# A hybrid diffusion layer on one core: Exp of the cumulated decay taken from the rows broadcast for the decays

## The chip, the cores and the metric

The kernel runs on one core of a Trainium2 chip. A core has five engines that run side by side, each through its own instructions in their fixed order: TensorE (PE: matmuls from the on-chip memory SBUF into the accumulation memory PSUM), VectorE (DVE), ScalarE (ACT), GpSimd (POOL) and SyncE (SP, which issues the DMA transfers here). They wait for each other through semaphores. The metric is the device time of one execution in microseconds (us).

## What is computed

One layer of a diffusion backbone for 512 latent tokens and 128 context tokens (640 columns, in five chunks of 128), 1024 channels. The part that the change touches is the Mamba-2 scan, with 16 heads of 64 channels, in two directions (forward and backward, d = 0 and 1):

```python
a_cum = jnp.cumsum(dtc * a.reshape(g, r), axis=2)             # per chunk of 128 tokens
seg = a_cum[:, :, :, None] - a_cum[:, :, None, :]
decay = jnp.exp(jnp.where(lower, seg, -jnp.inf))
cb = jnp.einsum("bcign,bcjgn->bcijg", cc, bc)
y_diag = jnp.einsum("bcijg,bcijgr,bcjgrp->bcigrp", cb, decay, xdt)
...
y_off = jnp.einsum("bcign,bcgrpn,bcigr->bcigrp", cc, prev, jnp.exp(a_cum))
y = (y_diag + y_off).reshape(bsz, seqlen, h, p).astype(x.dtype)
```

Around it stand an adaLN modulation, an input projection `proj = h @ prm["w_in"]` whose columns feed the scan and a gated convolution of 31 taps (with a layer norm over its channels), an output projection of both joined, and a gated feed-forward part with a 3x3 convolution between two products.

## The kernel before

Channels lie on the 128 partitions, tokens along the free dimension (640 columns). Each large product is made from splits of both operands into a high and a low part, with three matmuls for each k, in two halves of 384 and 256 columns (`mm3`, L261 to L267). The weights come in units: SP loads `wr` (L141), ScalarE rounds `wh` (L165), mostly POOL subtracts `wl` (L167). Three units may be split ahead.

The 16 heads are handled as eight pairs (p = 0 to 7), two heads h to a tile of 128 channels. `ssd(p)` (L584) does one pair. For each head and direction it broadcasts the row of the cumulated decay over all 128 partitions by a matmul with a selection column of `idr` (L623), in two pieces q of 384 and 256 columns; ScalarE takes Relu of the difference to the token's own decay, chunk by chunk (L629; for d = 1 of the last pair VectorE does, L626), then Exp of the whole row (L637). VectorE or POOL multiplies by the masked products of C and B (L640). L658 multiplies the result with the tokens: `y_diag`. The other term, `y_off`, is C times the states (L647), times `ea` (L649), both directions added (L650), and added to the rest by `ssd_tail` (L674). `ea` is exp(a_cum) with the two heads' values on the partitions of their channels. The inner function `decays()` makes it: VectorE casts a selection matrix `sel` (L600), one matmul of 512 columns for each direction broadcasts the rows by it (L604), and ScalarE takes Exp of each (L608).

Where tiles lie matters for the rest. The tiles `slot("S10")` and `slot("S11")` hold `ea` of every pair in turn; a new one can be written when L650 and L674 of the pair before have read the old one. PSUM has three large tiles of two banks each (P0, P1, P2; `ps0` to `ps2` in the listings) and two small banks (Q0, Q1; `pq0`, `pq1`). Pairs 0 to 6 broadcast their rows into Q0 and Q1 in turn. The last pair broadcasts into P0 (d = 0) and P2 (d = 1). P2 also holds the sums of the 31-tap convolution (`conv31`, L713), P1 the layer norm's statistics (`ln_stats`, L742: mean, the differences L752, their squares L754, the root L332 and the SiLU L827), and P0 is where six of the eight "ahead" products (`ahead_parts`, L843 to L850: the output projection's part for pairs 0 to 4, 30 matmuls to a unit) are summed; two go to P2.

The program is written pair by pair, with the projections between them (`seq`, L181 to L211), but the order in which each engine runs it is set when the kernel is built: a scheduler takes instructions as its own model of time says that they will be ready, so any change of the code can move instructions elsewhere. The order is then fixed.

Of the kernel before, what the change touches and what calls it, by code (L numbers as in the profile page):

```python
# [8 lines left out]
F32R = mybir.dt.float32r  # L9
AF = mybir.ActivationFunctionType  # L10
# [3 lines left out]
P = 128  # L14
D = 1024
L = 512
# [31 lines left out]
def hybrid_layer_kernel(ctx: ExitStack, tc: tile.TileContext, xT, ct, prm, cst, wrest, wdt, idhl_d, wada1, wada2, win,  # L48
                        wout, wup, wdown, st0, yT, nsf, nsb):
    nc = tc.nc  # L50
    te, ve, ac, gp, sy = nc.tensor, nc.vector, nc.scalar, nc.gpsimd, nc.sync
# [3 lines left out]
    sm = ctx.enter_context(tc.tile_pool(name="sm", bufs=2))  # L55
# [4 lines left out]
    def nm(s):  # L60
        uid[0] += 1
        return f"{s}_{uid[0]}"

    def slot(tag, dt=F32, shape=(P, T)):
        return sb.tile(list(shape), dt, tag=tag, name=nm(tag))

    def psum(i):
        return ps.tile([P, 1024], F32, tag=f"P{i}", name=nm(f"ps{i}"))

    def psq(i):  # L70
        return ps.tile([P, 512], F32, tag=f"Q{i}", name=nm(f"pq{i}"))
# [4 lines left out]
    def prm_col(name, i=0, n=1):  # L76
        a = _COLS[name][0] + i
        return prms[:, a:a + n]
# [25 lines left out]
    ids = sb.tile([P, 32], F32, tag="idhl", name="ids")  # L104
# [87 lines left out]
    for p in range(NPAIR):  # L192
# [4 lines left out]
        last = p == NPAIR - 1  # L197
# [345 lines left out]
    def ssd_tokens(p):  # L543

        xs = xsp[p]
        xt = xtp[p] = slot(("S14", "T13", "S14", "T13", "S14", "M2", "S14", "M2")[p])
        to_tokens(xs, xt)
        xw = []
        for d in range(2):
            o = slot(f"S{4 + d}")  # L550
            gp.tensor_tensor(hq(o), hq(xt), WD[:, :, 16 * d + 2 * p:16 * d + 2 * p + 2].unsqueeze(3)
                             .to_broadcast([P, NCH, 2, 64]), MUL)
            xw.append(o)
        xwp[p] = xw
# [29 lines left out]
    def ssd(p):  # L584
        g = p // 4
        xs, xt, prev = xsp[p], xtp[p], prevs[p]
        last = p == NPAIR - 1
        xd = []
        for d in range(2):
            o = slot(("M4", "H11")[d] if last else f"S{2 + d}")  # L590
            a = 16 * d + 2 * p
            gp.tensor_tensor(hq(o), hq(xt), DT[:, :, a:a + 2].unsqueeze(3).to_broadcast([P, NCH, 2, 64]), MUL)
            xd.append(o)

        ea = []

        def decays():
            peas = []
            sel = sm.tile([P, 2, 2, 64], F32R, tag="sel", name=nm("sel"), bufs=1)
            ve.tensor_copy(sel, ids.rearrange("p (d h) -> p d h", d=2)[:, :, 2 * p:2 * p + 2]  # L600
                           .unsqueeze(3).to_broadcast([P, 2, 2, 64]))
            for d in range(2):
                pea = psq(d)
                te.matmul(pea[:, 0:L], sel[:, d].rearrange("p h q -> p (h q)"), acHL[:, 0:L], start=True, stop=True)  # L604
                ea.append(slot(f"S{10 + d}"))
                peas.append(pea)
            for o, pea in zip(ea, peas):
                ac.activation(o[:, 0:L], pea[:, 0:L], AF.Exp)  # L608

        if last:  # L610
            decays()

        rs = {}
        for h in range(2):
            for d in range(2):
                row = 2 * p + h + 16 * d
                sel1 = idr[:, row:row + 1].to_broadcast([P, P])
                r = slot(f"{'H' if last else 'S'}{(12 if last else 6) + 2 * h + d}")
                if last:
                    pbl = psum(2 * d)  # L620
                for q, (c0, c1) in enumerate(((0, 3), (3, 5))):
                    pb = pbl[:, 512 * q:512 * q + 512] if last else psq(q)
                    te.matmul(pb[:, 0:(c1 - c0) * P], sel1, acHL[:, c0 * P:c1 * P], start=True, stop=True)  # L623
                    for c in range(c0, c1):
                        if last and d:
                            ve.tensor_scalar(r[:, c * P:(c + 1) * P], pb[:, (c - c0) * P:(c - c0 + 1) * P],  # L626
                                             ACM[:, c, row:row + 1], 0.0, SUB, MIN)
                            continue
                        ac.activation(r[:, c * P:(c + 1) * P], pb[:, (c - c0) * P:(c - c0 + 1) * P], AF.Relu,  # L629
                                      scale=-1.0, bias=ACM[:, c, row:row + 1])  # L630
                rs[h, d] = r
        if p + 1 < NPAIR:
            ssd_tokens(p + 1)
        if not last:
            decays()
        for (h, d), r in rs.items():
            ssd_exp[0] = ac.activation(r, r, AF.Exp, scale=1.0 if last and d else -1.0)  # L637
        for i, (h, d) in enumerate(rs):
            r = rs[h, d]
            (ve if i % 2 or last else gp).tensor_tensor(r, r, cbm[g][d], MUL)  # L640
        if p + 1 < NPAIR:
            ssd_states(p + 1)

        for d in range(2):
            po = psq(d)
            for c in range(4):
                te.matmul(po[:, c * P:(c + 1) * P], prev[d][c if d == 0 else 3 - c],  # L647
                          cT[g][:, c * P:(c + 1) * P], start=True, stop=True)
            ve.tensor_tensor(ea[d][:, 0:L], ea[d][:, 0:L], po[:, 0:L], MUL)  # L649
        (ve if p > 5 else gp).tensor_tensor(ea[0][:, 0:L], ea[0][:, 0:L], ea[1][:, 0:L], ADD)  # L650

        t = slot(f"T{p}")
        for q, cc in enumerate(((0, 1, 2, 3), (4,))):
            py = psq(q)
            for i, c in enumerate(cc):
                for d in range(2):
                    for h in range(2):
                        te.matmul(py[64 * h:64 * h + 64, i * P:(i + 1) * P],  # L658
                                  xd[d][:, c * P + 64 * h:c * P + 64 * h + 64],
                                  rs[h, d][:, c * P:(c + 1) * P], start=d == 0, stop=d == 1,  # L660
                                  tile_position=(0, 64 * h))
            c0, c1 = cc[0] * P, (cc[-1] + 1) * P
            ve.scalar_tensor_tensor(t[:, c0:c1], xs[:, c0:c1], prm_col("d_skip", p), py[:, 0:c1 - c0], MUL, ADD)
        yoff[p] = ea[0]
        tp[p] = t
# [105 lines left out]
    for it in seq:  # L771
        if it[0] == "proj":
            n = it[1]
# [3 lines left out]
            elif n[0] == "a":  # L777
                p = int(n[1:])
# [10 lines left out]
            elif n[:2] == "xs":  # L789
                p = int(n[2:])  # L790
# [12 lines left out]
        elif it[0] == "ssd":  # L803
            p = it[1]
# [362 lines left out]
    for i in range(HEAD, 2 * NF):  # L1167
        q, half = ups[i]
# [243 lines left out]
```

## Time and profile before

| | us |
|---|---|
| median of 3 runs | 1036.93 (1034.02 to 1041.4) |
| the profiled execution, whole | 1034.38 |
| its span on the core | 1032.6 |
| first part (norm, modulation, first projections) | 0 to about 80 |
| input projections and scan | about 80 to 422 |
| output projection and what follows | 422 to the end |

The whole execution is 1.8 us longer than the span, the time in which instructions run. In the listings, a group or line is named by its line in the kernel, the engine, the operation, and the tiles it writes and reads (out<-in, with their shape). Where idle time stands behind a row, it is that of the engine just before it, with what ended it.

### The profile page before, as it was taken

The numbers are of one execution on the slowest core, as the hardware profiler recorded it, in microseconds if no ns is written. First come the engines' busy times: TensorE is split into PE (matmuls) and PEld (weight loads), VectorE is DVE, ScalarE is ACT, GpSimd is POOL, SyncE is SP. The second block draws the span as 40 slices with busy tenths as digits, with TensorE's granted clock in tenths as the row PEclk, the third lists the DMA queues.
The fourth block names the chain that finished last, engine by engine and source line by source line (L and its number), as shares of the span: only waits on it lengthen the run. The fifth ranks groups of instructions, "written<-read, shape, count | busy, mean of one in ns | idle before, by whom it ended". The sixth has DMA issues, their size and how long they took to land. (4 is left out here: it accounts for less than half of the span.)

```text
span 1032.6 us, 18800 instructions
## 1 busy us (share of the span) xinstructions
PE 974.4 (94%) x7655; PEld 939.6 (91%) x7655; DVE 755.0 (73%) x1117; ACT 451.6 (44%) x750; POOL 574.3 (56%) x402
## 2 busy tenths in 40 slices
PE   4999999999999899999989969989999998999995
PEld 2799999999899888999889969989999998999995
DVE  3689999989999988762585999998888889200004
ACT  6244648565374677723455522323233336222221
POOL 3333878879778785543661535584444444344444
PEclk9999999999999999999999989989999999999998
DMA  9622222222111111588462311122222221222212
GB/s 344 233 67 78 68 72 63 72 67 68 52 62 57 50 39 47 196 293 292 133 207 86 121 62 62 63 68 76 82 64 81 83 81 55 62 90 72 68 46 102
DMA packets 42934, 102.76 MB, mean 100 GB/s; under 512 B 4832, under 2 KB 12768, under 8 KB 42848
## 3 DMA queue, kind: packets, MB, share of 16 engines
q1 hardware_dynamic: 42848, 101.56, 29.6%
q8 instruction: 60, 0.98, 0.4%
q14 instruction: 26, 0.21, 0.1%
HBM read 97.87 MB, written 3.67 MB: 98 GB/s over the span
## 5 line engine op out<-in xcount | busy, mean ns | idle before, releaser
L167 POOL TENSOR_TENSOR wl<-wr,wh 128x1024 fp32r<-128x1024 f32 (+3 forms) x127 | 301.8, 2378 | 306.5 <-ACT wh L165 300.5
L267 PE MATMUL ps<-H,wh 128*128 128x384 f32 (+1 forms) x1664 | 327.1, 310 | 4.9 <-DVE M L413 2.2
L267 PE MATMUL ps<-T,wh 128*128 128x384 f32 (+1 forms) x1504 | 283.9, 310 | 14.2 <-DVE S L1085 14.1
L165 ACT ACTIVATE wh<-wr 128x1024 fp32r<-128x1024 f32 (+3 forms) x131 | 131.6, 1005 | 335.9 <-PE ps L267 236.1
L267 PEld LDWEIGHTS ps<-H,wh 128*128 128x128 f32 x1664 | 253.0, 188 | 9.3 <-issue 4.5
L267 PEld LDWEIGHTS ps<-T,wh 128*128 128x128 f32 x1504 | 227.7, 190 | 15.3 <-issue 14.8
L1082 DVE SCALAR_TENSOR_TENSOR S<-ps,prms,S 128x441 f32<-128x441 f32 (+2 forms) x288 | 197.2, 692 | 28.4 <-ACT S L1072 22.1
L713 DVE SCALAR_TENSOR_TENSOR ps<-u,prms,ps 128x655 f32<-128x655 f32 x223 | 200.7, 900 | 9.9 <-ACT ps L710 5.4
L267 PE MATMUL ps<-H,wl 128*128 128x384 f32 (+1 forms) x832 | 197.9, 309 | 0.0
L267 PE MATMUL ps<-T,wl 128*128 128x384 f32 (+1 forms) x752 | 172.3, 309 | 0.0
L267 PEld LDWEIGHTS ps<-H,wl 128*128 128x128 f32 x832 | 130.9, 188 | 1.6 <-issue 1.4
L267 PEld LDWEIGHTS ps<-T,wl 128*128 128x128 f32 x752 | 116.8, 189 | 0.0
L333 DVE RECIPROCAL rsm<-rsm 128x160 f32<-128x160 f32 (+2 forms) x9 | 7.3, 815 | 145.4 <-ACT rsm L332 145.4
L267 PE MATMUL ps<-S,wh 128*128 128x384 f32 (+1 forms) x448 | 93.5, 315 | 4.0 <-DVE S L1085 3.3
L267 PEld LDWEIGHTS ps<-S,wh 128*128 128x128 f32 x448 | 71.0, 191 | 6.6 <-issue 4.7
L267 PE MATMUL ps<-S,wl 128*128 128x384 f32 (+1 forms) x224 | 58.3, 312 | 1.2 <-POOL wl L167 1.2
L629 ACT ACTIVATE S<-pq,ACM 128x128 f32<-128x128 f32 x140 | 40.9, 373 | 18.3 <-PE pq L623 18.1
L1082 DVE SCALAR_TENSOR_TENSOR S<-S,prms,S 128x441 f32<-128x441 f32 (+2 forms) x48 | 45.8, 984 | 1.2 <-ACT S L1072 1.1
L267 PEld LDWEIGHTS ps<-S,wl 128*128 128x128 f32 x224 | 37.6, 190 | 1.6 <-POOL wl L167 1.6
L1072 ACT ACTIVATE S<-ps,prms 128x640 f32<-128x640 f32 x36 | 31.3, 868 | 0.0
L1164 POOL TENSOR_TENSOR H<-S,S 128x640 f32<-128x640 f32 x16 | 26.0, 1622 | 3.3 <-DVE S L1085 3.3
L580 POOL TENSOR_TENSOR S<-S,stmp 128x128 f32<-128x128 f32 x36 | 18.6, 517 | 15.1 <-ACT S L569 11.2
(345 smaller groups left out, 1238.1 us busy)
## 6 DMA issues: line engine op xcount, KB each, us to landing
wr<-in_wup SPq DMA_DIRECT2D x44, 512.0 KB, 3.4
wr<-in_win SPq DMA_DIRECT2D x36, 512.0 KB, 3.4
T<-in_wada SPq DMA_DIRECT2D x49, 256.0 KB, 5.6
wr<-in_wdown SPq DMA_DIRECT2D x16, 512.0 KB, 3.4
wr<-in_wout SPq DMA_DIRECT2D x13, 512.0 KB, 3.4
H<-in_wada SPq DMA_DIRECT2D x23, 256.0 KB, 5.5
S<-in_wada SPq DMA_DIRECT2D x16, 256.0 KB, 5.5
wr<-in_wdown SPq DMA_DIRECT2D x8, 384.0 KB, 3.1
```

Source lines behind the costliest of these rows:

```text
L165: ac.activation(hi[:, :n], raw[:, :n], AF.Copy)
L167: lo_eng.tensor_tensor(lo[:, :n], raw[:, :n], hi[:, :n].bitcast(F32), SUB)
L267: last_mm[0] = te.matmul(pt[:, o:o + c1 - c0], w, x[:, c0:c1], start=first and i == 0, stop=last and i == 2)
L333: ve.reciprocal(r[:, 0:seg], r[:, 0:seg])
L580: gp.tensor_tensor(now, now, tmp, ADD)
L629: ac.activation(r[:, c * P:(c + 1) * P], pb[:, (c - c0) * P:(c - c0 + 1) * P], AF.Relu, scale=-1.0, bias=ACM[:, c, row:row + 1])
L713: ve.scalar_tensor_tensor(acc, u[:, j:j + UO], w(j), acc, MUL, ADD)
L1072: ac.activation(out, v, AF.Identity, bias=prm_col("ffn_b", i), scale=w(1, 1))
L1082: ve.scalar_tensor_tensor(ob, vl[:, r0 + a - 1:r1 + a - 1, q0 + b - 1:q1 + b - 1], w(a, b), ob, MUL, ADD)
L1164: gp.tensor_tensor(f_raw[q], a, b, MUL)
```

## The change

`decays()` goes, and with it the tile `sel`, its cast, the two selection matmuls of each pair and the two Exp of 512 columns. `ea` is taken instead from the rows that L623 broadcasts anyway: after the Relus on one piece of a row of head h and direction d, ScalarE takes Exp of the same PSUM bank on the 64 partitions of that head, for the columns of the latent tokens only: 384 in the first piece, 128 in the second. Each pair so has eight Exp of 64 partitions in place of two of 128. The slots S10 and S11 are taken at the start of `ssd`. For d = 1 of the last pair VectorE and ScalarE both read the row from PSUM.

```diff
-        ea = []
-
-        def decays():
-            peas = []
-            sel = sm.tile([P, 2, 2, 64], F32R, tag="sel", name=nm("sel"), bufs=1)
-            ve.tensor_copy(sel, ids.rearrange("p (d h) -> p d h", d=2)[:, :, 2 * p:2 * p + 2]
-                           .unsqueeze(3).to_broadcast([P, 2, 2, 64]))
-            for d in range(2):
-                pea = psq(d)
-                te.matmul(pea[:, 0:L], sel[:, d].rearrange("p h q -> p (h q)"), acHL[:, 0:L], start=True, stop=True)
-                ea.append(slot(f"S{10 + d}"))
-                peas.append(pea)
-            for o, pea in zip(ea, peas):
-                ac.activation(o[:, 0:L], pea[:, 0:L], AF.Exp)
-
-        if last:
-            decays()
+        ea = [slot(f"S{10 + d}") for d in range(2)]
...
                         ac.activation(r[:, c * P:(c + 1) * P], pb[:, (c - c0) * P:(c - c0 + 1) * P], AF.Relu,
                                       scale=-1.0, bias=ACM[:, c, row:row + 1])
+                    n = min(c1, 4) - c0
+                    hp = slice(64 * h, 64 * h + 64)
+                    ac.activation(ea[d][hp, c0 * P:(c0 + n) * P], pb[hp, 0:n * P], AF.Exp)
                 rs[h, d] = r
         if p + 1 < NPAIR:
             ssd_tokens(p + 1)
-        if not last:
-            decays()
```

The build gives the engines another order, mostly in small exchanges. The large move is at the end of the scan. Line numbers in the listings are those of each kernel's own file; in the changed one L608 is the row broadcast (L623 before), L614 the Relu (L629), L618 the new Exp, L623 the Exp of the row (L637), L633 the product with the states (L647), L836 the eviction of an ahead product (L850).

TensorE before, right after the last input projection: pair 7's rows for d = 0 go into P0 (`ps0_515`, `ps0_519`) between the work of pairs 5 and 6.

```order
L604 MATMUL pq1_424_3554<-HL_87_657,sel_421_3549 128x512
L623 MATMUL ps0_515_4279<-HL_87_657,idr_601 128x256
L565 MATMUL pq0_426_3567<-S4_419_3545,M7_292_2606 128x128 x3
L567 MATMUL pq0_426_3567<-M7_292_2606,S4_419_3545 128x128
L565 MATMUL pq1_428_3575<-S5_420_3547,M7_292_2606 128x128 x3
L567 MATMUL pq1_428_3575<-M7_292_2606,S5_420_3547 128x128
L623 MATMUL ps0_519_4297<-HL_87_657,idr_601 128x384
L647 MATMUL pq0_436_3601<-M5_237_2105,st_295_2616 128x128
L647 MATMUL pq0_436_3601<-M5_237_2105,S12_377_3145 128x128 x3
L647 MATMUL pq1_437_3607<-M5_237_2105,S13_379_3153 128x128 x3
L647 MATMUL pq1_437_3607<-M5_237_2105,st_295_2616 128x128
L623 MATMUL ps0_519_4297<-HL_87_657,idr_601 128x256
```

Sixteen small matmuls (L658) later the first ahead product follows in P0.

TensorE in the changed kernel, at the end of the scan, 79 rows after pair 7's first row broadcast into P0 (`ps0_491`); what stands between is small matmuls of pairs 5 to 7 and of the layer norm.

```order
L608 MATMUL ps2_493_4282<-HL_87_657,idr_601 128x256
L633 MATMUL pq0_498_4322<-M5_231_2105,st_386_3489 128x128
L633 MATMUL pq0_498_4322<-M5_231_2105,S12_455_3995 128x128 x3
L633 MATMUL pq1_499_4328<-M5_231_2105,S13_457_4003 128x128 x3
L633 MATMUL pq1_499_4328<-M5_231_2105,st_386_3489 128x128
L608 MATMUL ps0_491_4271<-HL_87_657,idr_601 128x256
L608 MATMUL ps2_497_4304<-HL_87_657,idr_601 128x384
L326 MATMUL ps1_485_4259<-rsm_484_4256,csts_85 128x160 x4
L608 MATMUL ps0_495_4293<-HL_87_657,idr_601 128x384
L608 MATMUL ps2_497_4304<-HL_87_657,idr_601 128x256
L608 MATMUL ps0_495_4293<-HL_87_657,idr_601 128x256
L267 MATMUL ps0_541_4477<-H0_504_4364,wh36_4064 128x384
```

The last row is the first ahead product: it moved from between pair 5's L658 to behind the last row of pair 7 and the layer norm's root.

ScalarE before, just after the last input projection: the Relus on pair 7's rows in P0 (`H12`, `H14`), pair 5's `ea` from the selection matmuls (S10, S11), then the first ahead product's eviction (L850).

```order
L629 ACTIVATE H12_514_4278<-ps0_515_4279,ACM_638 128x128 x3
L608 ACTIVATE S10_423_3553<-pq0_422_3551 128x512
L608 ACTIVATE S11_425_3556<-pq1_424_3554 128x512
L629 ACTIVATE H12_514_4278<-ps0_515_4279,ACM_638 128x128 x2
L637 ACTIVATE H12_514_4278<-H12_514_4278 128x640
L569 ACTIVATE S16_427_3572<-pq0_426_3567 128x512
L569 ACTIVATE AT_429_3580<-pq1_428_3575 128x512
L629 ACTIVATE H14_518_4296<-ps0_519_4297,ACM_638 128x128 x5
L637 ACTIVATE H14_518_4296<-H14_518_4296 128x640
L165 ACTIVATE wh39_4512<-wr39_4510 128x640
L850 ACTIVATE T0_566_4508<-ps0_565_4477 128x640
```

Here P0 is read by Relus alone, which wait for no other pair.

ScalarE in the changed kernel, at the end of the scan, from the layer norm's root on (the rows just ahead are the squares of L754, L740 there).

```order
L332 ACTIVATE rsm_484_4256<-ps1_474_4183,epsc_111 128x160
L618 ACT_TABLE_LOAD
L618 ACTIVATE S10_488_4268<-ps0_491_4271 64x384
L618 ACTIVATE S11_489_4269<-ps2_493_4282 64x128
L623 ACTIVATE H13_492_4281<-H13_492_4281 128x640
L614 ACTIVATE H12_490_4270<-ps0_491_4271,ACM_638 128x128 x2
L618 ACTIVATE S10_488_4268<-ps0_491_4271 64x128
L623 ACTIVATE H12_490_4270<-H12_490_4270 128x640
L663 ACTIVATE S9_471_4122<-T6_466_4037 128x640
L618 ACTIVATE S11_489_4269<-ps2_497_4304 64x384
L614 ACTIVATE H14_494_4292<-ps0_495_4293,ACM_638 128x128 x3
L618 ACTIVATE S10_488_4268<-ps0_495_4293 64x384
```

Pair 7's rows in P0 are now read to the end here, behind the layer norm's squares and pair 6; one more Relu pair and one Exp on `ps0_495` follow.

## The prediction

> **What bounds the kernel now.** I read the busy shares of the page first, then the stretches of the SSD part, then the order of time on each engine at its end. The first line is the share of each engine. The second is the stretch from 80 to 340 us (length, then busy time and instructions of TensorE, its weight loads, VectorE, ScalarE and POOL, then granted clock and DMA). The rows under it are stretches with TensorE alone.
>
> ```profile
> PE 974.4 (94%) x7655; PEld 939.6 (91%) x7655; DVE 755.0 (73%) x1117; ACT 451.6 (44%) x750; POOL 574.3 (56%) x402
> ...
> 80.00:340.00 260.00, 257.19 (x1928) 253.53 (x1927) 246.95 (x321) 145.77 (x291) 204.67 (x175) 1.00 0.20 65
> ...
> 348.00:360.00 12.00, 8.77 (x80) 1.00 0.16 50
> 360.00:380.00 20.00, 18.09 (x128) 1.00 0.11 34
> 380.00:400.00 20.00, 19.95 (x202) 1.00 0.16 51
> 400.00:422.00 22.00, 21.17 (x178) 1.00 0.38 122
> 606.00:610.00 4.00, 0.00 (x0) 0.79 0.00 0
> 610.00:614.00 4.00, 1.95 (x7) 0.50 0.00 0
> 700.00:720.00 20.00, 20.00 (x141) 1.00 0.19 63
> ```
>
> TensorE is the bound: from 80 to 340 us it stands still for 2.8 us of 260. The last input projection ends at 348; from there to 422 us no projection is left, and TensorE is kept busy only by the "ahead" products of L848, eight units of 30 matmuls, which run between the small matmuls of the last pairs. So this end of the SSD part depends on when the ahead products may start.
>
> ```profile
> 348.13 0.34 PE L623 MATMUL ps<-HL,idr 128*128 128x384 f32 x1
> ...
> 356.88 1.97 PE L658 MATMUL pq<-S,S 128*64 128x128 f32 x32 [2.37 <-DVE S L649]
> 358.78 0.85 PE L267 MATMUL ps<-H,wh 128*128 128x384 f32 x4
> ...
> 383.58 0.63 PE L604 MATMUL pq<-HL,sel 128*128 128x512 f32 x2
> 384.05 0.28 PE L267 MATMUL ps<-H,wh 128*128 128x256 f32 x1
> ...
> 421.73 1.45 PE L267 MATMUL ps<-S,wh 128*128 128x384 f32 x8 [0.47 <-ACT wh L165]
> ```
>
> The first ahead unit starts at 358.78 us, 10.7 us after the first row broadcast of pair 7 (348.13); the output projection proper starts at 421.73. From 348.1 to 421.7 it is 73.6 us, of which TensorE is idle for 6.0 by the stretches above.
>
> **The change, part by part.** The small edits first; the lines are groups (busy in total, mean ns).
>
> ```profile
> L600 DVE CAST sel<-ids 128x256 fp32r<-128x256 f32 x8 | 10.0, 1251 | 0.3 <-PE pq L604 0.3
> L608 ACT ACTIVATE S<-pq 128x512 f32<-128x512 f32 x16 | 8.7, 596 | 1.8 <-PE pq L604 1.8
> L629 ACT ACTIVATE S<-pq,ACM 128x128 f32<-128x128 f32 x140 | 40.9, 373 | 18.3 <-PE pq L623 18.1
> ```
>
> Removed on TensorE: 16 selection matmuls. They are pipelined, and two of them hold up the next matmul by 0.47 us (383.58 to 384.05), so 0.235 each: 3.8 us in all, and the 10 of pairs 0 to 4, which lie before 348 us where TensorE is full, give 2.35 us. Removed on VectorE: 8 casts, 10.0 us; VectorE is not what TensorE waits for before 348 us, so I count nothing for them there. Removed on ScalarE: 16 Exp, 8.7 us as groups count overlap. Added on ScalarE: 32 Exp of 64x384 and 32 of 64x128. No row has 64 partitions; the rows of 128 partitions give 0.37 for 128 columns and 0.60 for 512, and a straight line between them 0.52 for 384. Half of that is the other end, if partitions count. I take the full price, since the length of a row is what the two rows differ in: 32 x (0.52 + 0.37) = 28.5 us, a net 19.8 us more. Before 348 us ScalarE has 146 of 260 us busy, and the Exps lie behind Relus whose bank the next broadcast awaits only some microseconds later; I count nothing there, and price the opposite below.
>
> The large term is a wait that the change adds. Each Exp now reads the broadcast row in PSUM and writes S10 or S11. Both slots hold the products with the states of the pair before until that pair's L650 (S11) and L674 (S10) are done. For pairs 0 to 6 the rows lie in the small PSUM banks. For pair 7 they lie in P0 and P2, and P0 is the tile of the ahead products. Before, ScalarE emptied P0 by Relu alone, the last at 354.55, so that it was free at 355.2 us. Now pair 7's rows stay in P0 until pair 6 is through L674, and in the order of the changed kernel every ahead unit stands behind pair 7's last row. Behind the Exp that waits stand, on ScalarE in order, the root of the layer norm, pair 7's L637, the SiLUs of L827 and the splits of L165; TensorE waits for the release of P0 with all ahead units behind it, POOL's L167 for the splits, and SP's weight loads for their buffers (at a DMA share of 0.16 that costs nothing more). So I add up the chain from 348.1 us to the release of P0, with nothing large on TensorE meanwhile.
>
> ```profile
> 351.70 1.63 DVE L600 CAST sel<-ids 128x256 fp32r<-128x256 f32 x1
> ...
> 354.55 0.62 ACT L629 ACTIVATE H<-ps,ACM 128x128 f32<-128x128 f32 x2 [0.83 <-PE ps L623]
> ...
> 356.15 0.68 DVE L649 TENSOR_TENSOR S<-S,pq 128x512 f32<-128x512 f32 x1
> ...
> 363.96 1.29 POOL L674 TENSOR_TENSOR T<-T,S 128x512 f32<-128x512 f32 x1
> ...
> 368.73 0.74 ACT L677 ACTIVATE S<-T 128x640 f32<-128x640 f32 x1 [1.31 <-POOL T L675]
> ...
> 372.42 0.92 ACT L629 ACTIVATE S<-pq,ACM 128x128 f32<-128x128 f32 x3
> ...
> 373.79 0.69 ACT L629 ACTIVATE S<-pq,ACM 128x128 f32<-128x128 f32 x2
> 374.51 0.74 ACT L637 ACTIVATE S<-S 128x640 f32<-128x640 f32 x1
> ...
> 377.48 0.31 ACT L747 ACTIVATE mean<-ps 128x160 f32<-128x160 f32 x1
> ...
> 379.81 0.75 ACT L438 ACTIVATE M<-pq 128x512 f32<-128x512 f32 x2
> ...
> 380.92 3.07 POOL L551 TENSOR_TENSOR S<-M,WD 128x640 f32<-128x640 f32 x2
> ...
> 381.25 11.34 DVE L752 TENSOR_TENSOR T<-T,U 128x640 f32<-128x640 f32 x8
> ...
> 391.14 1.07 ACT L569 ACTIVATE S<-pq 128x512 f32<-128x512 f32 x2
> ...
> 394.70 1.27 DVE L649 TENSOR_TENSOR S<-S,pq 128x512 f32<-128x512 f32 x2
> 396.01 0.96 DVE L650 TENSOR_TENSOR S<-S,S 128x512 f32<-128x512 f32 x1
> ...
> 399.03 1.00 DVE L663 SCALAR_TENSOR_TENSOR T<-S,prms,pq 128x512 f32<-128x512 f32 x2
> 399.94 0.68 DVE L674 TENSOR_TENSOR T<-T,S 128x512 f32<-128x512 f32 x1
> ...
> 398.27 1.28 ACT L332 ACT_TABLE_LOAD   x1
> 399.56 0.40 ACT L332 ACTIVATE rsm<-ps,epsc 128x160 f32<-128x160 f32 x1
> ...
> 409.58 0.91 ACT L827 ACTIVATE T<-T,prms 128x640 f32<-128x640 f32 x1
> ```
>
> Leg 1, to pair 5's L674 on POOL. It ended at 365.25. The cast of 351.70 (1.63 us) stood ahead of L649 (356.15) on VectorE and goes; L649 still needs its matmuls, so I take 1.4 us of it as a gain: 363.8.
> Leg 2, pair 6's four rows. Each is three Relus 0.9, Exp 0.52, two Relus 0.65, Exp 0.37, the Exp of L637 0.74: 3.2 us. The first row's Relus run before S10 is free, so 0.9 + 3 x 3.2, and L677 (0.74) and a tanh of z about as long between them, 1.4: 375.8.
> Leg 3, tokens of pair 7 (0.75), one product of L551 (1.5), its state matmuls and their eviction (L569, 0.54, so about 0.9 with the matmuls): the mean at 378.9. From the mean to the first L752 took 3.77 us before (377.48 to 381.25): 382.6.
> Leg 4, on VectorE: L752 11.34, one L649 of 0.64, L650 0.96, L663 1.00, L674 0.68: 397.2.
> Leg 5, on ScalarE from the last L752 (394.6): a square 0.74, an Exp 0.52, the table and root of L332 1.68, a table again 1.28 (398.8); then four Exps of 384 or 128 columns for the first rows and the second, five Relus, two L637, L677 and three Exps more, in all about 7.1: P0 is free at 405.9.
>
> That is 57.8 us after 348.1, where it was 10.7. The rest follows. The price of an ahead matmul is 20.00/141 = 0.142 us, so eight units take 34.1 us; pair 7's L658 (1.97 us for 32 rows above, 40 rows a pair, so 2.5). To this come four waits for ScalarE, counted from the release of P0. The first unit's eviction (0.68) comes behind two L637, an Exp, a table, five SiLUs (0.82 each) and a split (0.74): done at 8.7, when TensorE could go on at 6.8: 1.9. The second follows its unit directly: 1.0. Behind it come a table, the root, a table, five SiLUs and the split for the next weights, at 21.8, when the third unit has ended at 18.3: 3.5. The fourth stands behind one more SiLU: 0.9. Together 7.3. So the output projection starts 43.9 us after 405.9, at 449.8 instead of 421.7: 28.1 us later, less 2.35: 25.7. After it nothing changes, as TensorE has almost no idle time (0.47 us) at the seam that could take this in. The sum is 1034.4 of the profiled execution (span 1032.6) + 25.7 = 1060.1 us; the median shown is 1036.9, 2.5 above that execution, so I predict 1062.6.
>
> A table load costs 1.28 us in these rows: the root of 399.56 starts as the load of 398.27 ends. The Trainium skill (ScalarE: Activation LUTs, section "What ACT_TABLE_LOAD costs") puts a switch at 2.66 us, a drain of 1.38 included; by that the two switches of leg 5 would add an estimated 2.8 us and the result would be about 1065. The row shows no drain, and I keep it.
>
> Bounds. On VectorE the changed order has between pair 5's first L649 and the end of pair 6's L674: 16 of L713, L752 11.34, four L649 2.5, two pairs of L663 2.0, L650 and L674 1.6, and smaller ones that I put at 5.
>
> ```profile
> L713 DVE SCALAR_TENSOR_TENSOR ps<-u,prms,ps 128x655 f32<-128x655 f32 x223 | 200.7, 900 | 9.9 <-ACT ps L710 5.4
> ```
>
> With 16 x 0.90 = 14.4 that is 36.8 us of work; from 356.15 - 1.63 = 354.5 it ends at 391.3, and leg 5 puts P0 8.7 behind: not before 400.0, 5.9 less. Without any of the four waits the second part is 7.3 shorter; the idle 2.8 before 340 us could vanish or double. Low end 1062.6 - 5.9 - 7.3 - 2.8 = 1046.6; above, some 3 us for handovers that I didn't count, 2.8, and the clock below, 6.8: 1075.
>
> **Rivals.** (a) The clock drops in the bare stretch. At 612 us TensorE starts again after a gap, and the stretches 606:610 and 610:614 above show 0.79 and 0.50; the gap of 2.37 at 356.88 left 1.00.
>
> ```profile
> 612.05 1.41 PE L267 MATMUL ps<-T,wh 128*128 128x384 f32 x4 [8.30 <-DVE S L1085]
> ```
>
> From 358 to 364 us TensorE would have nothing to do, and later it runs a few small matmuls per microsecond or two. If it meets the first ahead units at half speed, once or twice for the 6.8 us or so that 606 to 614 suggests, each time costs up to 3.4: about 1069. The Trainium skill (TensorE: Matmul & The Clock Gate, section "What's actually happening") says that one idle window of about 3.4 us halves the clock; the two gaps agree, and a stretch that is only thinly busy is shown by no run here.
>
> (b) Not slower: P0 is emptied without waiting for pair 6, or pair 6 is through early. It decides if P0 is free by 405.9 - 25.7 = 380.2 us. For it: VectorE loses 10.0 us of casts. Against: pair 6's row exponentials alone reach 375.8, and L752 stands ahead of L674 on VectorE. Then the saved matmuls remain: 1036.9 - 3.8 = 1033; a middle case ends near 1040.
>
> (c) ScalarE late everywhere: the banks of the broadcast rows are held longer by 0.37 to 0.52 and TensorE stands at each of the 40 broadcasts of pairs 0 to 4: 18 us more, 1080. Against it: in 1928 matmuls up to 340 us there are only 2.8 us of idle time.
>
> **How the numbers follow.** My forecast holds with 0.66, (a) 0.14, (b) 0.12, (c) 0.08. The likeliest gives 1062.6. The range 1047 to 1076 leaves out (b) and (c), 0.20. About 1% is what a measurement of this kernel can tell from no change: faster by more 0.03, within it 0.09 (both from (b)), slower 0.88 (the rest).
>
> **What would show it.** In the changed profile: ahead products of L848 begin near 405 us and not near 359; TensorE is busy for less than half of the time from 346 to 404; the Exps of pair 7 on P0 wait for VectorE's L674 or stand behind its neighbours; the part before 346 us is about 2 us shorter; and from the output projection on the two traces run alike. If the ahead products start before 390 us, leg 4 or 5 was too long; if TensorE idles before 346 us, it is (c); if the clock is below 1.00 around 405 us, (a).

## The result

The changed kernel takes 1072.99 us (median of 4 runs, 1070.39 to 1078.3); the kernel before took 1037.08 (4 runs, 1034.02 to 1041.4). The ratio is 1.035, with a 95% interval of 1.029 to 1.041: 36 us slower, 30 to 42 by the interval. The profiled execution of the changed kernel took 1078.3 us, its span is 1076.5, which is 43.9 more than the 1032.6 of before.

The shares of the engines alone tell little. This is TensorE's share on the page of the changed kernel:

```profile
PE 995.3 (92%) x7639; PEld 957.3 (89%) x7639; DVE 733.1 (68%) x1109; ACT 467.6 (43%) x798; POOL 572.9 (53%) x402
```

TensorE has 16 instructions fewer and is busy 20.9 us longer, since its matmuls ran at a lower pace in places, which the rows below show. VectorE has 21.9 us less to do, ScalarE 16.0 more.

TensorE's rows of the changed kernel in order of time (start, duration, engine, line, out<-in, shape, count; in brackets the idle time just before and what ended it):

```profile
87.07 0.57 PE L478 MATMUL pq<-T,csts 128*128 128x80 f32 x4
...
357.79 0.34 PE L608 MATMUL ps<-HL,idr 128*128 128x384 f32 x1
...
365.16 4.54 PE L644 MATMUL pq<-S,S 128*64 128x128 f32 x40 [3.37 <-DVE S L635]
...
374.00 0.68 PE L608 MATMUL pq<-HL,idr 128*128 128x384 f32 x2 [3.28 <-ACT S L618]
...
386.67 1.65 PE L565 MATMUL pq<-S,M 128*128 128x128 f32 x6 [2.42 <-POOL S L551]
...
411.24 0.38 PE L608 MATMUL ps<-HL,idr 128*128 128x256 f32 x1 [1.02 <-ACT S L618]
412.63 1.43 PE L267 MATMUL ps<-H,wh 128*128 128x384 f32 x4 [1.01 <-ACT S L618]
...
459.44 0.74 PE L267 MATMUL ps<-S,wh 128*128 128x384 f32 x4
```

The first row is the first matmul of the cumulated decay; of the change only one cast of `sel` lies ahead of it (on VectorE, at 20.5 us of the kernel before). The row at 357.79 is pair 7's first broadcast into P0, that at 412.63 the first ahead product, that at 459.44 the first matmul of the output projection. The same four places were at 82.74, 348.13, 358.78 and 421.73 before. The eleven microseconds between pair 7's first row and the first ahead product have become 54.8.

Stretches of the changed kernel there (length, busy time and instructions of TensorE, its weight loads, VectorE, ScalarE and POOL, granted clock, DMA share, GB/s):

```profile
360.00:380.00 20.00, 9.98 (x63) 7.54 (x62) 18.18 (x23) 8.76 (x25) 17.84 (x21) 0.69 0.10 30
380.00:400.00 20.00, 14.85 (x135) 11.08 (x135) 13.17 (x19) 10.51 (x23) 14.40 (x17) 0.72 0.03 8
400.00:412.60 12.60, 7.98 (x63) 5.42 (x62) 11.74 (x21) 11.96 (x24) 0.00 (x0) 0.83 0.00 1
412.60:420.00 7.40, 7.37 (x32) 7.17 (x32) 4.43 (x8) 6.62 (x9) 1.24 (x1) 0.59 0.00 0
420.00:440.00 20.00, 16.57 (x144) 14.96 (x144) 12.29 (x19) 17.96 (x25) 10.28 (x7) 1.00 0.42 122
440.00:459.40 19.40, 19.40 (x136) 19.02 (x135) 12.46 (x9) 8.21 (x13) 9.90 (x6) 1.00 0.51 156
```

Up to 412.6 us TensorE does small matmuls between waits, and its clock falls. The DMA share falls to nothing too: SP issues no transfer from 392.3 to 420.4 us, and the next load of a weight at 422.2. From 440 us on TensorE is full again.

The second place that lost time is the long stretch before, from the first L478 to pair 7's first row. First the kernel before, then the changed one, both over exactly that stretch:

```profile
82.74:348.13 265.39, 262.58 (x1966) 258.91 (x1966) 251.88 (x327) 152.89 (x307) 207.03 (x177) 1.00 0.20 65
```

```profile
87.07:357.79 270.72, 262.73 (x1956) 259.68 (x1956) 235.73 (x314) 164.63 (x345) 207.50 (x177) 0.99 0.20 63
```

It takes 5.3 us longer: TensorE's idle time has grown from 2.8 to 8.0 us. Its busy time is the same although it has 10 matmuls less, since behind two of the waits below (those of 1.9 and 2.1 us) its matmuls ran at half speed for some microseconds. ScalarE has 11.7 us more work, VectorE 16.2 less. The changed kernel's waits of TensorE in it (line waiting, tile, what was waited for, total, times, longest):

```profile
PE pq L436 <- ACT S L618: 2.6, 1, 2.6
PE pq L516 <- DVE T L649: 2.1, 1, 2.1
PE ps L267 <- DVE M L413: 1.9, 1, 1.9
PE ps L267 <- ACT u L678: 1.2, 1, 1.2
```

The longest is for a new Exp (L618), which holds a small bank that the transposes of L436 need.

So the 43.9 us between the two spans are made of four parts: 4.3 before the first L478; 5.3 from there to pair 7's first row; 28.1 from that to the output projection (101.65 where it was 73.60); and 6.2 behind it (617.1 where it was 610.9). The first has one instruction of the change in it, that cast, and the last has none; what is known of them is told under the hardware. The two others, 33.4 us, hold all the rest of the change, and they lie inside the 30 to 42 of the ratio. The parts are those of one execution each, and that of the changed kernel was the slowest of its four, which is why they sum up to more than the 36 us between the medians.

### The profile page after: what moved, and what is told of

The parts are those of the page before. It is cut to its first block, busy times and chain, and to the rows that moved or that the text cites. A ratio compares the mean times of both kernels' runs of the same rounds, so it can differ in the third digit from the quotient of the medians.

```text
span 1076.5 us, 18792 instructions
## 1 busy us (share of the span) xinstructions
PE 995.3 (92%) x7639; PEld 957.3 (89%) x7639; DVE 733.1 (68%) x1109; ACT 467.6 (43%) x798; POOL 572.9 (53%) x402
## 5 line engine op out<-in xcount | busy, mean ns | idle before, releaser
L167 POOL TENSOR_TENSOR wl<-wr,wh 128x1024 fp32r<-128x1024 f32 (+3 forms) x127 | 301.7, 2378 | 337.8 <-ACT wh L165 331.8
L267 PE MATMUL ps<-T,wh 128*128 128x384 f32 (+1 forms) x1504 | 288.3, 313 | 16.0 <-DVE S L1071 15.9
L267 PEld LDWEIGHTS ps<-H,wh 128*128 128x128 f32 x1664 | 257.2, 191 | 13.8 <-issue 6.2
L267 PEld LDWEIGHTS ps<-T,wh 128*128 128x128 f32 x1504 | 230.0, 190 | 17.1 <-issue 16.6
L267 PE MATMUL ps<-T,wl 128*128 128x384 f32 (+1 forms) x752 | 174.7, 312 | 0.0
L614 ACT ACTIVATE S<-pq,ACM 128x128 f32<-128x128 f32 x140 | 42.0, 365 | 34.2 <-PE pq L608 33.9
L1144 ACT ACTIVATE S<-S 128x640 f32<-128x640 f32 x21 | 15.4, 734 | 27.0 <-DVE S L1071 17.0
```

The source lines that it names most:

```text
L167: lo_eng.tensor_tensor(lo[:, :n], raw[:, :n], hi[:, :n].bitcast(F32), SUB)
L267: last_mm[0] = te.matmul(pt[:, o:o + c1 - c0], w, x[:, c0:c1], start=first and i == 0, stop=last and i == 2)
L1144: ac.activation(a, a, AF.Silu)
```

## The experiments

Theory H, the prediction's: pair 7's rows stay in P0 until pair 6 has given S10 and S11 back, and this makes the loss. Rival C: the Exps on 64 partitions load ScalarE, and the loss comes from that wherever they stand. The time of one kernel differs by up to 14 us between executions (the kernel before took 1031.42 to 1045.32 beside e1), so the two stretches of the profile are the finer measure: where the code in them is the same, the first repeats within 0.8 us. For every kernel, from its TensorE rows in order of time:

| kernel | L478 to pair 7's first row | from there to the output projection |
|---|---|---|
| before | 265.4 | 73.6 |
| changed | 270.7 | 101.7 |
| e1_last_old | 270.9 | 72.9 |
| e2_only_last | 265.5 | 100.0 |
| e3_own_slots | 271.3 | 83.4 |
| e4_one_exp | 271.4 | 80.7 |
| e5_exp_first | 270.7 | 80.7 |
| e6_after_exp_first | 270.7 | 101.4 |
| e7_twice | 283.0 | 81.2 |
| e8_short | 261.6 | 71.7 |
| e9_reads_first | 271.3 | 80.5 |
| e10_pool_cast | 267.8 | 77.2 |
| e11_three_tiles | 270.5 | 79.1 |
| e12_tiles_reads | 270.5 | 76.1 |

Each kernel has line numbers of its own.

**Pair 7 alone, and all but pair 7 (e1, e2).** In e1 `decays()` is kept for the last pair:

```diff
         if last:
             decays()
+        else:
+            ea = [slot(f"S{10 + d}") for d in range(2)]
...
+                    if last:
+                        continue
                     ac.activation(ea[d][hp, c0 * P:(c0 + n) * P], pb[hp, 0:n * P], AF.Exp)
```

> Pairs 0 to 6 as in the changed kernel, pair 7 with the selection matmuls and the Exp from the small banks as before. Theory H (the whole loss is that pair 7's rows stay in P0 until pair 6 gives S10 and S11 back): the ahead products start about 11 us after pair 7's first row again, and what is left is the 5.3 us that the changed kernel's profile lost between 87 and 358 us: 1037 + 5 = 1042 us, at best 1035. Rival C (the 64 Exps on 64 partitions load ScalarE, and the loss comes from that wherever they stand): seven eighths of the Exps are still here, so 1065 us or more.

Measured: 1041.26 us beside 1041.99 for the kernel before, ratio 1.002 (0.998 to 1.006). The second stretch is that of before (72.9), the first that of the changed kernel (270.9). H holds, C falls as the cause of the large part. The 5.5 us of the first stretch don't show in the whole time, but the interval of the ratio, 2 us less to 6 us more, doesn't exclude them.

In e2 the condition is turned round: only pair 7 takes the Exp from its rows.

> The converse: pairs 0 to 6 as before, pair 7 alone takes its Exp from the broadcast rows in P0 and P2. Theory H: the stretch without large products is there as in the changed kernel, 44 us longer up to the first ahead product and 16 us shorter behind it: 1037 + 28 = 1065 us. Rival C: one eighth of the Exps, so 1037 to 1042 us.

Measured: 1058.68 us, ratio 1.017 (1.011 to 1.023). The second stretch is 100.0 us, 26.4 more than before, the first 265.5 as before. H holds by the stretches. The whole time falls short of them: 17 us more than the kernel before beside it (11 to 24 by the interval), where 28 were expected. The first ahead product of e2, on TensorE:

```profile
402.56 1.44 PE L267 MATMUL ps<-H,wh 128*128 128x384 f32 x4 [1.01 <-ACT S L635]
```

It stands 53.3 us behind pair 7's first row (349.26), waits for the last Exp on P0 (L635 there), and runs at half speed, as in the changed kernel. The two stretches add up: 5.5 (e1) and 26.4 (e2) make 31.9, against 33.4 with both.

**Pair 7 in tiles of its own (e3), and one Exp per row (e4).** If pair 6's slots are the hold, other tiles must undo it:

```diff
-        ea = [slot(f"S{10 + d}") for d in range(2)]
+        ea = [slot(("H10", "M3")[d] if last else f"S{10 + d}") for d in range(2)]
...
-            sq = slot(("U1", "M3", "S17")[p % 3])
+            sq = slot(("U1", "S17")[p % 2])
```

> All pairs as in the changed kernel, but pair 7 writes its Exps to two tiles that are free by then (H10 and M3; the squares of the layer norm then take two tiles in turn instead of three), so they don't wait for pair 6. No work is left out. Theory H: P0 is free some microseconds after its rows, the ahead products run between the small matmuls again: 1040 to 1044 us, as with pair 7 of the old kind. Rival S (ScalarE is late for P0 in any case, since it has the Exps of both pairs and the layer norm in order): the stretch stays over 35 us long and the time over 1058 us.

Measured: 1060.76 us, ratio 1.017 (1.009 to 1.024): a miss by 17 us. Yet the hold is gone: the first ahead product starts 10.7 us behind pair 7's first row, as before. The stretch is 18.3 us shorter than in the changed kernel and still 10.5 longer than with the old pair 7. So H is right on the place and not the whole: something else holds pair 7. (A part of the miss lies behind the output projection, which takes 619.4 us here and 610.9 before; 6.1 of that is the second pace told at the end.) ScalarE's longest wait in the stretch, in e3's order of time:

```profile
404.91 0.49 ACT L618 ACTIVATE M<-ps 64x384 f32<-64x384 f32 x1 [7.34 <-DVE H L611]
```

and VectorE's rows around it:

```profile
392.81 11.29 DVE L738 TENSOR_TENSOR T<-T,U 128x640 f32<-128x640 f32 x8
404.02 0.85 DVE L611 TENSOR_SCALAR H<-ps,ACM 128x128 f32<-128x128 f32 x3
```

The Exp reads a row in P2 that VectorE reads as well (L611). It waits until VectorE has read it, though neither writes it, and VectorE first does the layer norm's eight subtractions. By the Trainium skill (PSUM — Partial Sum Buffer, section "PSUM bank collisions raise a hardware error") two engines must not touch one bank in the same partition at once, reads included, and the compiler's scheduler orders such accesses; the wait in this row agrees.

e4 is e3 with another cut of the rows:

```diff
-                for q, (c0, c1) in enumerate(((0, 3), (3, 5))):
+                for q, (c0, c1) in enumerate(((0, 4), (4, 5))):
...
+                    if q == 0:
+                        hp = slice(64 * h, 64 * h + 64)
+                        ac.activation(ea[d][hp, 0:L], pb[hp, 0:L], AF.Exp)
```

> As the run with tiles of their own for pair 7, and each row is broadcast as 512 and 128 columns instead of 384 and 256, so that one Exp of 64x512 replaces one of 64x384 and one of 64x128. 32 Exps fewer, each 0.27 us: ScalarE has 8 us less. If the loss of some 5 us in pairs 0 to 5 comes from late Exps, part of it goes: 2 to 5 us below the run with tiles of their own. If it is only what one execution differs from another by, the two are within 2 us.

Measured: 1058.35 us, 2.4 below e3, with a first stretch of 271.4 where e3 has 271.3. The first stretch didn't gain, which speaks against the theory that the run was made for; but the cut of the rows also changes how long each small bank is held, and the two were not taken apart.

**What is left in the stretch of pair 7 (e5, e6, e9, e11, e12).** e5 issues these Exps of pair 7 ahead of VectorE's reads, in e3's tiles; e6 does so in the changed kernel, in S10 and S11:

```diff
                     te.matmul(pb[:, 0:(c1 - c0) * P], sel1, acHL[:, c0 * P:c1 * P], start=True, stop=True)
+                    ex = lambda: ac.activation(ea[d][hp, c0 * P:(c0 + n) * P], pb[hp, 0:n * P], AF.Exp)
+                    if last and d:
+                        ex()
...
+                    if not (last and d):
+                        ex()
```

> As the run with tiles of its own for pair 7, but in pair 7's second direction, where VectorE reads the row and not ScalarE, the Exp is issued ahead of VectorE's four reads. In the run before, the Exp at 404.91 us waited 7.34 us for VectorE's reads, which stood behind the eight subtractions of the layer norm. Theory V (this wait is what is left of the loss in the stage of pair 7, which took 83.4 us from its first row to the output projection against 72.9 with the old pair 7): the Exp waits for the matmul alone, and the stage takes 73 to 77 us. Rival L (ScalarE's work and its place among the evictions is what is left): 80 to 85 us.

> The changed kernel with the same Exps ahead of VectorE's reads, and pair 7 still in S10 and S11. Theory H (the slots of pair 6 are the hold): the stage of pair 7 stays at 96 to 102 us. If the order of the readers of P2 is the hold by itself: 85 us or less.

e6: 101.4 us in the stretch, as H has it, and 1072.20 us in one run; the order of P2's readers is not the hold of the changed kernel. e5: 80.7, and 1052.5 us in all (ratio 1.014, 1.008 to 1.021). V falls, as 80.7 lies in the range of its rival: the wait only moved on by one instruction on ScalarE, to the Exp of the row that VectorE's reads make (L627 in e5):

```profile
405.05 0.74 ACT L627 ACTIVATE H<-H 128x640 f32<-128x640 f32 x1 [7.07 <-DVE H L616]
```

So e9 moved VectorE's reads as well, by a higher priority on them, and e11 and e12 undid a side edit of e3, the two tiles for the squares where there had been three:

```diff
+                            with tc.high_priority(offset=300):
                                 ve.tensor_scalar(r[:, c * P:(c + 1) * P], pb[:, (c - c0) * P:(c - c0 + 1) * P],
                                                  ACM[:, c, row:row + 1], 0.0, SUB, MIN)
...
-            sq = slot(("U1", "S17")[p % 2])
+            sq = slot(("U1", "S4", "S17")[p % 3])
```

> As the run with the Exps ahead of VectorE's reads, and these reads of pair 7's second direction are given a higher priority, so that on VectorE the last two of the first row stand behind three of the layer norm's eight subtractions and not behind all eight. In the run before, ScalarE stood 7.07 us at 405.05 for these two reads. Theory V2 (VectorE's order at this place makes the rest of the loss): the wait shrinks to about 2 to 3 us and the stage of pair 7 falls from 80.7 to 74 to 77 us. Rival: the stage stays at 79 to 82, and the wait turns up at another place.

> As the run with the Exps ahead of VectorE's reads (stage of pair 7: 80.7 us), but the squares of the layer norm have three tiles in turn again (S4 in the place of M3). No work is left out. Theory D (the two tiles, an edit of the experiments and not of the change, made ScalarE's squares wait for TensorE's sums over partitions, and the root of the layer norm and all SiLUs come late with them): the stage falls to 74 to 78 us. Rival: 79 to 82, and what is left of the loss is the change's own.

> Both: three tiles for the squares, and VectorE's reads of pair 7's second direction ahead of five of the eight subtractions. If the two causes hold the same place one after the other: 72 to 75 us for the stage, as with the old pair 7 (72.9), and 1042 to 1045 us in all, from the 5.5 us of pairs 0 to 6. If neither is it: 79 to 82 us and 1050 to 1054.

Measured: e9 80.5 (1052.98 us, ratio 1.012, 1.005 to 1.020), e11 79.1 (1057.76 in one run), e12, with both, 76.1 (1052.45, ratio 1.016, 1.007 to 1.025). In e9 the wait at that place shrank to 1.10 us and the stretch stayed: V2 falls too as a cause by itself, and so does D, which gave 1.6. Together they give 4.6, more than the sum, which fits two holds of the same chain of ScalarE (squares, root and SiLU): in e9 ScalarE stands 3.98 us ahead of a square at 408.56 instead, and in e11 5.75 us at 403.11 for VectorE's reads. But e12 reached neither the 72 to 75 us nor the 1042 to 1045 that were expected, and ScalarE still stands 3.04 us ahead of a square at 408.15, by no releaser that the profile shows. 3.1 us more than with the old pair 7 remain, and what they are stays open.

**The first stretch (e7, e8).** On e1, the Exps of pairs 0 to 6 doubled (e7), and cut to 16 columns (e8; shown without the products with the states, which take these columns repeated):

```diff
-                    ac.activation(ea[d][hp, c0 * P:(c0 + n) * P], pb[hp, 0:n * P], AF.Exp)
+                    ac.activation(ea[d][hp, L + 16 * q:L + 16 * q + 16], pb[hp, 0:16], AF.Exp)
```

> Pair 7 of the old kind, and in pairs 0 to 6 every Exp on 64 partitions is issued twice, with the same result. The stretch from the first matmul of the cumulated decay (L478) to pair 7's first row took 265.4 us before and 270.9 in three kernels with the new Exps. Theory E (the time of the Exps on ScalarE, while they hold the small banks, makes those 5.5 us): the same again or more, 274 to 285 us. Rival O (the order that the list of instructions came out in makes them, and ScalarE has room): 269 to 272.

> Pair 7 of the old kind; in pairs 0 to 6 each Exp takes 16 columns instead of 384 or 128, and the products with the states are multiplied by those 16 columns repeated, so most of the decay factors are left out. Theory E: most of the Exps' time is gone and the stretch from L478 to pair 7's first row falls from 270.9 to about 263 to 266 us. Rival O: 269 to 272.

The stretch in e8, then in e7 (columns as above):

```profile
82.08:343.65 261.57, 260.83 (x1965) 257.97 (x1964) 245.43 (x321) 153.48 (x343) 210.86 (x179) 1.00 0.21 66
```

```profile
83.70:366.67 282.97, 264.99 (x1948) 259.06 (x1947) 243.09 (x322) 168.68 (x363) 202.89 (x175) 0.97 0.20 61
```

In one run each they took 1025.84 us (e8, most of the decay factors left out) and 1083.98 (e7). TensorE's idle time in the stretch is 0.7 us with 16 columns, 8.1 with the whole Exps (e1) and 18.0 with two of each. The stretch follows the Exps' time, as theory E has it: 283.0 lies in its range and 261.6 under it, and of e7's idle time 9.4 us, in four waits, end with an Exp that holds the bank of the next row's broadcast. In e8 the 48 Exps in it take 8.4 us of ScalarE, in the changed kernel 18.1, and the stretch is 9.1 us shorter. These are their groups, first in e8, then in the changed kernel (busy in all, mean ns):

```profile
L637 ACT ACTIVATE S<-pq 64x16 f32<-64x16 f32 x48 | 8.4, 176 | 0.4
```

```profile
L618 ACT ACTIVATE S<-pq 64x384 f32<-64x384 f32 (+1 forms) x48 | 18.1, 379 | 0.4
```

Yet E isn't shown to be the whole. The build put the instructions of this stretch in another order in e7 and in e8 than in e1, while TensorE, ScalarE and POOL have one and the same order there in e1, in e3 and in the changed kernel; so rival O isn't excluded. And e4, with 7.0 us less work on ScalarE than e1, is no shorter: its idle time on TensorE is 2.1 us less, its busy time 2.6 more. The stretch in e1, then in e4:

```profile
83.20:354.07 270.87, 262.80 (x1956) 259.28 (x1956) 242.06 (x320) 164.67 (x345) 207.35 (x177) 0.99 0.21 64
```

```profile
86.42:357.83 271.41, 265.41 (x1951) 261.73 (x1951) 239.88 (x313) 157.71 (x315) 204.47 (x176) 0.99 0.20 63
```

e7 shows one thing more: its second stretch is 81.2 us, though its pair 7 is of the old kind. More Exps in pairs 5 and 6 lengthen that stretch too.

**The other half of the change alone (e10).** The kernel before, with GpSimd in VectorE's place for the eight casts:

```diff
-            ve.tensor_copy(sel, ids.rearrange("p (d h) -> p d h", d=2)[:, :, 2 * p:2 * p + 2]
+            gp.tensor_copy(sel, ids.rearrange("p (d h) -> p d h", d=2)[:, :, 2 * p:2 * p + 2]
```

> The kernel before, with one thing of the change's aim: VectorE is spared the eight casts of the selection columns, which GpSimd does instead. The changed kernel's gain (casts off VectorE) without its cost (Exps on 64 partitions, the wait for pair 6). If VectorE's casts cost TensorE anything: the stretch from L478 to pair 7's first row falls from 265.4 by 1 to 3 us, and the time is 1034 to 1037 beside 1037. If not, or if GpSimd is late with them: 265 to 268 us and no difference that can be measured.

Measured: 1050.75 us beside 1043.09, ratio 1.007 (1.003 to 1.011); the stretches are 267.8 and 77.2, each longer than before. Taking the casts off VectorE this way costs about 0.7%. No kernel of the study that does the whole computation beats the one before; e1 comes out even with it.

## Why the prediction came out as it did

The sign, the place and most of the size were right: 1062.6 us predicted, 1072.99 measured, inside 1047 to 1076. That it is inside is in part luck: of the 43.9 us between the two profiled executions 28.1 came where they were forecast; 5.3 came from a term that was forecast as a gain of 2.35, and 10.5 in places where no change was forecast. Term by term, against the changed kernel's profiled execution (us; the length of a stretch, before, predicted and measured):

| term | before | predicted | measured |
|---|---|---|---|
| up to pair 7's first row, change | | -2.35 | +5.3 from L478, and 4.3 ahead of it |
| pair 7's first row to the first ahead product | 10.7 | 57.8 | 54.8 |
| first ahead product to the output projection | 62.9 | 43.9 | 46.8 |
| output projection to the end, change | | 0 | +6.2 |

**The wait for pair 6.** The two stretches together were predicted at 101.7 us and are 101.65; e2 shows the wait by pair 7 alone, e3 that it goes when the slots are others. That the sum agrees so closely is luck: its two parts are off by 3.0 us and 2.9 us, one down and one up, and so are the legs. TensorE was also busier than the prediction's sign had it (less than half of the time): for 32.8 of the 52.6 us from 360 to 412.6, with its small matmuls at half speed for much of them. The rows on which the legs end, first POOL's, then VectorE's, then ScalarE's, all of the changed kernel in order of time:

```profile
372.16 1.27 POOL L660 TENSOR_TENSOR T<-T,S 128x512 f32<-128x512 f32 x1
```

```profile
394.38 1.83 DVE L738 TENSOR_TENSOR T<-T,U 128x640 f32<-128x640 f32 x2 [1.14 <-ACT U L736]
...
399.55 2.28 DVE L738 TENSOR_TENSOR T<-T,U 128x640 f32<-128x640 f32 x3
401.75 0.68 DVE L636 TENSOR_TENSOR S<-S,S 128x512 f32<-128x512 f32 x1
...
403.27 0.68 DVE L660 TENSOR_TENSOR T<-T,S 128x512 f32<-128x512 f32 x1
```

```profile
383.75 0.74 ACT L623 ACTIVATE S<-S 128x640 f32<-128x640 f32 x1
...
402.59 0.47 ACT L618 ACTIVATE S<-ps 64x384 f32<-64x384 f32 x1
403.08 1.28 ACT L332 ACT_TABLE_LOAD   x1
404.37 0.39 ACT L332 ACTIVATE rsm<-ps,epsc 128x160 f32<-128x160 f32 x1
404.78 1.28 ACT L618 ACT_TABLE_LOAD   x1
406.08 0.65 ACT L618 ACTIVATE S<-ps 64x384 f32<-64x384 f32 x2
...
412.31 0.27 ACT L618 ACTIVATE S<-ps 64x128 f32<-64x128 f32 x1
```

Counted from pair 7's first row (357.79; 348.1 in the prediction):
- Leg 1, pair 5's L674, now L660 on POOL: ends 15.6 us behind it, predicted 15.7.
- Leg 2, pair 6's rows: L623 ends at 26.7, predicted 27.7.
- Leg 3, the first subtraction: 36.6, predicted 34.5. Pair 7's states waited for POOL (2.42 us at 386.67).
- Leg 4, pair 6's last L660: ends at 46.2, predicted 49.1. The eight subtractions (L738) were done in 7.5 us, from 394.38 to 401.83, where the prediction took over 11.34 from the row of before. In e3 they took 11.29, in the order of before again. One by one, a subtraction took 0.81 us with nothing on POOL beside it (in the kernel before and in the changed one), 0.8 to 1.1 beside POOL's small products (changed kernel, e3), and 1.6 to 2.2 beside its large ones, L551, L592 and L167 (before, e3). So a duration from a stretch where POOL is busy is not that of one where it is idle.
- Leg 5: P0 free for the first ahead product at 54.8, predicted 57.8. The two table loads cost 1.28 each, and the root starts as its load ends; the drain that the Trainium skill (ScalarE: Activation LUTs, section "What ACT_TABLE_LOAD costs") counts with a load is not in these rows, neither ahead of the loads nor behind them.

The Exp on S11 at 402.59 starts 0.16 us behind the end of L636, which read S11, and that on S10 follows L660 and the table: the slots of pair 6, as predicted. ScalarE isn't idle ahead of the first, though; it comes right behind the eight squares. The hold shows as the place that the build gave these Exps, not as a wait for the slot, and that the slots are the reason for the place is shown by e3.

**The second part.** Of the 7.3 us of waits for ScalarE that were predicted, 3.4 came (the idle time between 420 and 440 us). In their place came rival (a): the clock stood at 0.59 from 412.6 to 420 us, and 32 matmuls took 7.37 us there, 2.8 more than at 0.142 each. The prediction gave (a) 3.4 us for each time and a chance of 0.14. With 34.1 and 2.5 for the matmuls these make 42.8 of the 46.8 us; the other 4.0 hold the small matmuls between the ahead units (L318, L848, L308), for which the prediction's sum has no term.

**The step that failed** is one of size, up to pair 7's first row: "I count nothing there" for the Exps of pairs 0 to 6, since ScalarE had 146 of 260 us busy and the next broadcast came some microseconds later. That ScalarE is idle for 114 us didn't help at the three places where TensorE waited 1.9 to 2.6 us, once for an Exp and twice for VectorE; with the short Exps of e8 none of the three is left, and its longest wait there is 0.6 us. By e8 against before, dropping matmuls and casts is worth 3.8 us there (2.35 predicted for the matmuls), and by the changed kernel against e8 the Exps cost 9.1, not 0, as far as the order, which differs too, lets one say. Rival (c) priced this at 18 us, by a wait at each of 40 broadcasts; half of that came, in a few long waits of which one ends with an Exp, and not instead of the forecast but beside it.

The price of one Exp was taken high, 0.52 and 0.37 us; the rows show 0.485 and 0.273 (13.6 us for 28 and 7.6 for 28). The length of a row is the price, and 64 partitions are no cheaper than 128: in e4 64x512 took 0.595, and the row of before with 128x512 had 0.596.

Rival (b), not slower, needed P0 free 32.1 us behind pair 7's first row; it was 54.8.

## What to carry to other kernels

When a value is to be taken from a buffer that is there anyway, ask what the new reader waits for: here it waited for its own output tile, and so the buffer, and all that was queued for it, waited for the pair before. Give such a reader an output tile that is free at that time, or leave it a buffer of its own, as the selection matmuls did. And work added to an engine that is idle for 44% of a stretch need not be free: here 9.7 us of Exps more on ScalarE went with 9.1 us more of the stretch, where each Exp stands between a full buffer and its release.

## What the runs showed of the hardware

**The clock falls on short waits and in thin stretches.** In the first stretch of the changed kernel a wait of 1.93 us was enough:

```profile
189.95 1.40 PE L267 MATMUL ps<-H,wh 128*128 128x384 f32 x4 [1.93 <-DVE M L413]
191.15 0.73 PE L267 MATMUL ps<-H,wl 128*128 128x384 f32 x2
191.68 1.27 PE L267 MATMUL ps<-H,wh 128*128 128x384 f32 x4
192.75 0.73 PE L267 MATMUL ps<-H,wl 128*128 128x384 f32 x2
193.28 0.79 PE L267 MATMUL ps<-H,wh 128*128 128x384 f32 x4
```

Four matmuls take 1.40 us in place of 0.74, and the full pace is back 3.3 us later. The 2.37 us of before, ahead of the row at 356.88, had no such effect. Many short waits do it too. From 397 to 401.7 us TensorE counts as busy for 59% of the time and no wait is longer than 0.58 us; then the clock is halved for 3.4 us (the two stretches, and the row with that wait):

```profile
397.00:401.70 4.70, 2.79 (x48) 1.05 (x46) 4.70 (x6) 3.44 (x5) 1.78 (x3) 0.99 0.01 2
401.70:405.10 3.40, 3.17 (x28) 2.08 (x25) 3.16 (x8) 3.35 (x6) 0.00 (x0) 0.52 0.02 5
```

```profile
398.51 0.48 PE L318 MATMUL ps<-S,ones 128*32 128x160 f32 x8 [0.58 <-ACT S L740]
```

The Trainium skill (TensorE: Matmul & The Clock Gate, section "What's actually happening") ties the halved clock to an idle window of about 3.4 us in a free-running grid; the length of the halved phase agrees, but in these rows waits shorter than the window halve the clock.

**The same matmuls at two paces.** The products behind the feed-forward convolution are 1248 matmuls in every kernel here. Their stretch before, in the changed kernel, in e12 and in e11:

```profile
691.30:877.00 185.70, 182.42 (x1248) 181.99 (x1248) 165.30 (x266) 65.05 (x80) 85.29 (x40) 0.98 0.23 75
```

```profile
728.70:920.50 191.80, 188.66 (x1248) 188.40 (x1248) 165.39 (x266) 65.00 (x80) 84.93 (x40) 0.99 0.23 73
```

```profile
705.70:888.70 183.00, 179.73 (x1248) 179.29 (x1249) 165.30 (x266) 65.10 (x80) 85.34 (x40) 1.00 0.24 76
```

```profile
707.50:900.40 192.90, 189.70 (x1248) 189.48 (x1248) 165.46 (x266) 65.00 (x80) 84.96 (x40) 0.98 0.23 72
```

The stretch takes 183 to 186 us in nine of the fourteen profiles and 191.7 to 192.9 in five (the changed kernel, e3, e4, e7, e11), with 3.1 to 3.3 us of idle time and at a granted clock of 0.98 to 1.00 in both: 0.144 to 0.146 us for a matmul, or 0.151 to 0.152. Neither the place of the tiles nor the Exps tell the two apart, as e6, which is the changed kernel but for the order of four Exps, shows 184.5. It makes 6.1 of the 6.2 us that the changed kernel's profile lost behind the output projection. Its cause stays open.

**The part ahead of the first L478** differs too. It takes 82.1 to 83.8 us in the five kernels that cast a `sel` on VectorE in it (before, e1, e2, e7, e8) and 84.9 to 87.6 in the nine others. VectorE's order differs between these groups as well, so the 4.3 us may be the change's by way of the build; no run shows it.
